# Every other piece of the experts' weights is issued by ScalarE instead of SyncE

## The chip, the cores and the metric

The kernel runs on one core of a Trainium2 chip. The metric is the device time of one execution in microseconds (us). The core has TensorE (PE) for matrix products, VectorE (DVE), ScalarE (ACT), GpSimd (POOL) and SyncE (SP). Each has its own queue of instructions, which it works off in order; a transfer (DMA) is an instruction in the queue of the engine that issues it, and runs on the core's 16 DMA engines once it is issued.

## The reference

One token sequence of 256 rows and 1024 columns, all in float32, runs through a hybrid layer (attention beside a gated delta rule), and then through a second block: two kinds of attention, a mixture of 32 experts of which each token takes four, an added embedding, and a last norm. What matters here is the mixture and what follows it:

```python
logits = xt @ w_router + b_router
top_logit, top_e = lax.top_k(logits, 4)
gate = softmax(top_logit)
# for the tokens xs of one expert e:
hh = xs @ w_gu[e] + b_gu[e]                  # w_gu[e]: 1024 x 2048
glu, lin = jnp.split(hh, 2, axis=-1)
glu = jnp.minimum(glu, 7.0); lin = jnp.clip(lin, -7.0, 7.0)
act = glu * sigmoid(1.702 * glu) * (lin + 1.0)
y = act @ w_dn[e] + b_dn[e]                  # w_dn[e]: 1024 x 1024
# y times its gate is added to the token's row; then, for all tokens:
u = rmsnorm(h, g_ple)
h = h + sigmoid(u @ w_ple_gate) * (p @ w_ple_proj)
out = rmsnorm(h, g_final)
```

An expert has 12 MiB of weights, the 32 of them 384 MiB, and each is read once.

## The kernel before

**Units and pieces.** The experts are worked off in 17 units. Most units are two experts side by side with up to 64 tokens each ("pair"); the first and the one at place 15 hold a single expert. The generator `pieces` gives the weights in the order in which they are needed, in pieces of 1 MiB (128 partitions x 2048 numbers): for unit i the 8 pieces per expert of w_gu, then for unit i - 1 the 4 per expert of w_dn. A pair has 16 and 8, so 24 pieces go by from one unit to the next. With one piece of w_ple_proj at i = 12 (`EMB`) there are 385, p0 to p384. From the fourth expert on, the place of an expert's weights comes from a register: `in_register` loads it from the tile `eidi` on SyncE.

**Slots.** `load` (line 103) puts piece after piece into 15 buffers in turn; the names raw, whi and wlo are the tiles whose room is reused for that. `ahead` fills the first eleven while the router still runs; in `run`, `refill` issues as many pieces as there are free slots after each group of products (`products`, recorded in line 1363). Every piece is issued by SyncE in line 116. A transfer's instruction waits for the product that last read its slot, and, as the eight semaphores for transfers are taken in turn, for the landing of the piece eight before it. So no more than eight are in flight.

**One unit on the engines.** TensorE multiplies the tokens by the w_gu pieces into four accumulators (ph), and ScalarE and VectorE copy those to hs (line 1550). While the products of the w_dn pieces of the unit before run (pm), nothing else is wanted of ScalarE. Behind the last of them comes a boundary: ScalarE writes yh, the result times its gate (line 1452), and VectorE the rest yl (line 1453); TensorE gathers the tokens of the unit after next, which ScalarE copies to xs (line 1386); hs is transposed, and `activation` runs on VectorE and ScalarE (sw, act; lines 1432 to 1443); TensorE adds yh and yl to the tokens' rows (`combine`, ohT), and VectorE to hres (line 1464). Then the next w_gu products start. A scheduler sets the order in which these stand on each engine; it is fixed when the kernel is built.

**The end.** Behind the last unit all engines load a register from novi and branch on it (`further`, a loop for tokens beyond 64 per expert, which these inputs don't enter). The gate projection that follows needs w_ple_gate in four pieces, each split into two parts of less precision: a cast on ScalarE (whi, line 315) and a subtraction on VectorE (wlo, line 316). Its products stand in lines 158 to 160.

Of the kernel before, what the change touches and what calls it, by code (L numbers as in the profile page):

```python
# [15 lines left out]
P = 128  # L16
S = 256
D = 1024
# [49 lines left out]
def tile_net(ctx: ExitStack, tc: tile.TileContext, a: dict, dbg=None):  # L68
    nc = tc.nc
    V, A, G, T, SY = nc.vector, nc.scalar, nc.gpsimd, nc.tensor, nc.sync  # L70
# [30 lines left out]
    def slots():  # L101
        return sum(n_ for _, _, n_ in raws)

    def load(src, kc, n, pool=None, rows="(k p) n -> p k n"):

        if pool is None:
            i = count[0] % slots()
            count[0] += 1
            for pool, name, nb in raws:
                if i < nb:  # L110
                    break
                i -= nb
        else:
            (pool, nb), name = pool, "raw"
        raw = pool.tile([P, 2048], F32, name=name, bufs=nb)
        SY.dma_start(raw[:, :kc * n].rearrange("p (k n) -> p k n", k=kc), src.rearrange(rows, p=P))
        return raw

    def piece(src, kc, n, raw=None, by=None):
# [13 lines left out]
    def rows_piece(W, i, pool=None):  # L133
        nh, k0 = i // 2, (i % 2) * 4
        return load(W[k0 * P:(k0 + 4) * P, nh * 512:(nh + 1) * 512], 4, 512, pool)
# [270 lines left out]
    with ExitStack() as c1:  # L406
# [16 lines left out]
        for i in (2, 1):  # L423
# [3 lines left out]
        rows = [("conv_w", 96), ("gdn_norm_w", 1), ("g_cq_2", 3), ("g_ckv_2", 2),  # L427
                ("g_out_mla_2", 4), ("g_out_sb_2", 4), ("g_attn_2", 8), ("g_ple_2", 8)]
        vr = wk.tile([P, P], F32, name="vrow1")
        at = 0  # L430
        for n, k in rows:
            voff[n] = 16 + at
            src = a[n]
            src = src.rearrange("o t (c p) -> (o t c) p", p=P) if n == "conv_w" else src.rearrange("o (c p) -> (o c) p", p=P)
# [678 lines left out]
    NE = 32  # L1113
# [6 lines left out]
    def pieces(units):  # L1120


        for i in range(len(units) + 1):
            if i < len(units):
                rs = [p["row"]() for p in units[i]["places"]]
                for k in range(8):
                    for r in rs:
                        yield wgu[bass.ds(r + k * P, P)], 1, 2 * D, "(k p) n -> p k n"
            if i:
                rs = [p["row"]() for p in units[i - 1]["places"]]  # L1130
                for q in range(4):
                    for r in rs:
                        yield wdn[bass.ds(r + q * 2 * P, 2 * P)], 2, D, "(p k) n -> p k n"
            if i == EMB:
                yield a["w_ple_proj_2"][0], 2, D, "(k p) n -> p k n"

    def ahead_or_none(order):
        for src, kc, m, rows in order:
            return load(src, kc, m, None, rows), kc, m

    def ahead(order, n, pool=None):

# [2 lines left out]
    def in_register(ap):  # L1145

        r = []

        def row():
            if not r:  # L1150
                r.append(nc.values_load(ap, engines=[mybir.EngineType.SP], min_val=0, max_val=NE - 1) * D)
            return r[0]
        return row

    with ExitStack() as c3:
# [31 lines left out]
        def unit(ps_, i):  # L1187


            return dict(places=ps_, at=i)  # L1190
# [264 lines left out]
        def combine(b, tiles=(0, 1)):  # L1455
            for t in tiles:
                pss = [pm.tile([P, 512], F32, name="pm") for _ in range(2)]
                for nh in range(2):
                    ns = slice(nh * 512, nh * 512 + 512)
                    for i, y in enumerate(b["y"]):  # L1460
                        mm(pss[nh], b["oh"][:, t], y[:, ns], start=i == 0, stop=i == 1)
                for nh in range(2):
                    o = hres[:, t, nh * 512:nh * 512 + 512]
                    V.tensor_tensor(o, o, pss[nh], ALU.add)  # L1464
                yield

        def bias_of(ev):
            br = wk.tile([P, 512], F32, name="sw", bufs=4)[:8, :2 * P]
            SY.dma_start(br, a["b_gu_2"][0].rearrange("e (q f) -> e q f", f=2 * P)[bass.ds(ev, 1)].rearrange("o q f -> (o q) f"))
            ps = pm.tile([P, 2, 8], F32, name="pm")  # L1470
            for k in range(2):
                turn_(ps[:, k], br[:, k::2])
            bi = wk.tile([P, 16], F32, name="bie")
            V.tensor_copy(bi.rearrange("p (q k) -> p k q", k=2), ps)
            return bi
# [132 lines left out]
        def further():  # L1608

            every = raws[:]  # L1610
            raws[:] = raws[:1]
            count[0] = 0
            with tc.If(nov[0] > 0):
                with tc.For_i(0, nov[0]) as jv:
                    ji = wk.tile([P, 2], I32, name="ji")
                    cur = wk.tile([P, 2, 2], F32, name="cur")
                    oh = wk.tile([P, NE], F32, name="oh")
                    x1 = wk.tile([P, NE], F32, name="x1")
                    bs = wk.tile([P, 2], F32, name="bs")
                    jf = wk.tile([P, 1], F32, name="jf")  # L1620
                    V.tensor_copy(jf, iota16[:, bass.ds(jv, 1)])
                    V.tensor_scalar(x1, st0, jf, None, ALU.is_le)
                    V.scalar_tensor_tensor(oh, ce, jf, x1, ALU.is_gt, ALU.mult)

                    V.tensor_scalar(x1, st0, jf, -64.0, ALU.subtract, ALU.mult)
                    V.scalar_tensor_tensor(x1, o0, 64.0, x1, ALU.mult, ALU.add)
                    V.tensor_scalar(x1, x1, 65.0, None, ALU.add)
                    V.tensor_tensor(x1, x1, oh, ALU.mult)
                    V.tensor_reduce(bs[:, 0:1], x1, AX.X, ALU.add)
                    V.tensor_tensor(x1, oh, iota32, ALU.mult)  # L1630
                    V.tensor_reduce(bs[:, 1:2], x1, AX.X, ALU.add)
                    V.tensor_copy(ji, bs)
                    for t in range(2):
                        V.tensor_tensor(x1, oh, selp[:, t], ALU.mult)
                        V.tensor_reduce(cur[:, 0, t:t + 1], x1, AX.X, ALU.add)
                        V.tensor_tensor(x1, oh, gate[:, t], ALU.mult)
                        V.tensor_reduce(cur[:, 1, t:t + 1], x1, AX.X, ALU.add)
                    V.tensor_scalar(cur[:, 0], cur[:, 0], bs[:, 0:1], None, ALU.subtract)
                    ej = nc.values_load(ji[0:1, 1:2], engines=[mybir.EngineType.SP], min_val=0, max_val=NE - 1)
                    bi = bias_of(ej)  # L1640
                    one = [unit([dict(row=lambda: ej * D, v=[lambda t: cur[:, 0, t:t + 1]],
                                      g=lambda t: cur[:, 1, t:t + 1], bias=lambda: bi)], 0)]
                    for _ in combine(run(one, pieces(one), [], None, (("hs", 2), ("hs", 2)))):
                        pass
            raws[:] = every
# [124 lines left out]
```

## Time and profile before

| what | before |
|---|---|
| median of 3 runs | 1566.31 us (1565.58 to 1567.18) |
| the profiled execution | 1564.52 us, of which its span (first to last instruction) 1562.7 us |
| mean granted clock of TensorE | 0.985 |
| TensorE busy | 1427.0 us (91%) |
| VectorE, ScalarE busy | 618.7 us (40%), 415.6 us (27%) |
| transfer queue (SyncE's) | 485.87 MB, 78.3% of 16 engines' span |

The profile is one execution. A share of busy time is a mean over stages that differ: up to about 550 us the hybrid layer, the attention and the router run, from there to about 1520 us the experts, then the embedding's gate and the last norm. Busy time doesn't say what an engine waits for; the lists of waits and the order in time say that, and the slices of the span say in which stage.

### The profile page before, as it was taken

Reading aid. Unit: us, or ns where it says so; the run is one execution under the profiler, and the core shown is the slowest. Engines: PE = TensorE matmul, PEld = TensorE weight load, DVE = VectorE, ACT = ScalarE, POOL = GpSimd, SP = SyncE. Lnnn points to the kernel's source line nnn. Section 1 sums busy time; section 2 is a strip of 40 time slices with the busy share of each in tenths; the row PEclk is TensorE's granted clock in tenths of the full one; section 3 lists DMA queues with packets and bytes.
Section 4 is the critical chain, followed back from the end, with each engine's and each line's share of the span. In section 5 each row is a group of like instructions: output and inputs, shape, how many; then the busy total and the mean of one; then the engine's idle time right before and its main releaser. Section 6 shows DMA issues by size and latency. Waiting matters only on the chain. (4 is left out here: it accounts for less than half of the span.)

```text
span 1562.7 us, 20025 instructions
## 1 busy us (share of the span) xinstructions
PE 1427.0 (91%) x7922; PEld 872.8 (56%) x7922; DVE 618.7 (40%) x1215; ACT 415.6 (27%) x636; POOL 27.1 (2%) x39
## 2 busy tenths in 40 slices
PE   6999998999889999998989988999998899897887
PEld 5889898999788865443433332444343244242235
DVE  6868865556556651330221330231223022122126
ACT  5543654444457521110110110111011011011014
POOL 0000100000000000000000000000000000000000
PEclk9999999999999989999999999999999999999998
DMA  7544244355354199999999999999999999999982
GB/s 241 165 150 150 89 143 130 108 189 201 100 165 136 54 379 393 421 421 421 421 421 420 421 422 421 420 421 421 421 421 421 421 420 422 421 421 421 421 336 88
DMA packets 108541, 487.58 MB, mean 312 GB/s; under 512 B 14766, under 2 KB 23356, under 8 KB 59292
## 3 DMA queue, kind: packets, MB, share of 16 engines
q1 hardware_dynamic: 108300, 485.87, 78.3%
q8 instruction: 64, 1.05, 0.3%
q0 software_dynamic: 144, 0.39, 0.1%
q14 instruction: 33, 0.27, 0.0%
HBM read 483.48 MB, written 2.75 MB: 311 GB/s over the span
## 5 line engine op out<-in xcount | busy, mean ns | idle before, releaser
L1363 PE MATMUL ph<-raw,xs 128*64 128x512 f32 x928 | 233.9, 597 | 7.3 <-DMA raw<-in_w_gu_dram 7.3
L1363 PE MATMUL ph<-whi,xs 128*64 128x512 f32 (+1 forms) x568 | 192.8, 594 | 1.4 <-DMA whi<-in_w_gu_dram 1.3
L316 DVE TENSOR_TENSOR wlo<-raw,whi 128x2048 fp32r<-128x2048 f32 (+4 forms) x73 | 158.0, 2165 | 87.9 <-ACT whi L315 87.7
L1363 PE MATMUL ph<-wlo,xs 128*64 128x512 f32 (+1 forms) x552 | 187.1, 594 | 3.2 <-DMA wlo<-in_w_gu_dram 3.2
L212 PE MATMUL pm<-w,wlo 128*128 128x256 f32 x640 | 179.9, 282 | 6.9 <-DVE wlo L316 6.9
L210 PE MATMUL pm<-w,whi 128*128 128x256 f32 x640 | 182.6, 286 | 3.3 <-ACT whi L315 3.3
L1550 DVE COPY hs<-ph 128x512 f32<-128x512 f32 x34 | 23.5, 691 | 405.4 <-PE ph L1363 405.4
L211 PE MATMUL pm<-w,whi 128*128 128x256 f32 x640 | 180.4, 282 | 0.3 <-DVE w L316 0.3
L315 ACT CAST whi<-raw 128x2048 fp32r<-128x2048 f32 (+4 forms) x73 | 132.0, 1808 | 135.8 <-PE pm L211 83.9
L1363 PE MATMUL pm<-raw,act 128*64 128x512 f32 x528 | 146.3, 597 | 22.7 <-DMA raw<-in_w_dn_dram 22.0
L1363 PEld LDWEIGHTS ph<-raw,xs 128*64 128x64 f32 x928 | 75.0, 138 | 143.0 <-issue 126.1
L1550 ACT COPY hs<-ph 128x512 f32<-128x512 f32 x34 | 19.9, 585 | 413.6 <-PE ph L1363 413.6
L1453 DVE SCALAR_TENSOR_TENSOR yl<-pm,gs,yh 128x512 fp32r<-128x512 f32 x34 | 25.5, 749 | 262.0 <-ACT yh L1452 261.2
L212 PEld LDWEIGHTS pm<-w,wlo 128*128 128x128 f32 x640 | 122.3, 192 | 8.1 <-DVE wlo L316 8.0
L210 PEld LDWEIGHTS pm<-w,whi 128*128 128x128 f32 x640 | 122.2, 191 | 4.1 <-ACT whi L315 3.9
L211 PEld LDWEIGHTS pm<-w,whi 128*128 128x128 f32 x640 | 122.3, 191 | 0.8 <-DVE w L316 0.7
L1363 PEld LDWEIGHTS ph<-whi,xs 128*64 128x64 f32 (+1 forms) x568 | 61.9, 140 | 83.0 <-issue 78.4
L1363 PEld LDWEIGHTS ph<-wlo,xs 128*64 128x64 f32 (+1 forms) x552 | 59.3, 140 | 84.7 <-issue 76.8
L1363 PE MATMUL pm<-wlo,act 128*64 128x512 f32 (+1 forms) x248 | 94.2, 597 | 13.0 <-DMA wlo<-in_w_dn_dram 13.0
L1363 PE MATMUL pm<-whi,act 128*64 128x512 f32 (+1 forms) x248 | 92.4, 596 | 13.2 <-DMA whi<-in_w_dn_dram 13.2
L1363 PEld LDWEIGHTS pm<-raw,act 128*64 128x64 f32 x528 | 44.0, 136 | 102.3 <-issue 59.9
L1452 ACT ACTIVATE yh<-pm,gs 128x512 fp32r<-128x512 f32 x34 | 23.4, 687 | 279.0 <-PE pm L1363 277.2
(394 smaller groups left out, 1921.7 us busy)
## 6 DMA issues: line engine op xcount, KB each, us to landing
raw<-in_w_gu_dram SPq DMA_DIRECT2D x116, 1024.0 KB, 19.8
whi<-in_w_gu_dram SPq DMA_DIRECT2D x71, 1024.0 KB, 19.8
wlo<-in_w_gu_dram SPq DMA_DIRECT2D x69, 1024.0 KB, 19.8
raw<-in_w_dn_dram SPq DMA_DIRECT2D x66, 1024.0 KB, 19.8
raw<-in_w_in_dram SPq DMA_DIRECT2D x46, 1024.0 KB, 5.9
wlo<-in_w_dn_dram SPq DMA_DIRECT2D x31, 1024.0 KB, 19.8
whi<-in_w_dn_dram SPq DMA_DIRECT2D x31, 1024.0 KB, 18.6
raw<-in_w_branch_a_dram SPq DMA_DIRECT2D x4, 1024.0 KB
```

The source lines that it names most:

```text
L210: T.matmul(o, hi[:, k, ns], xh[:, k0 + k], start=first, stop=False)
L211: T.matmul(o, hi[:, k, ns], xl[:, k0 + k], start=False, stop=False)
L212: T.matmul(o, lo[:, k, ns], xh[:, k0 + k], start=False, stop=last)
L315: A.copy(hi, src)
L316: (by or V).tensor_tensor(lo, src, hi.bitcast(F32), ALU.subtract)
L1363: return tc.keep_in_program_order(T.matmul(*x_, **y_))
L1452: A.activation(yh[:, ns], yp[n_], AF.Copy, scale=b["gs"])
L1453: V.scalar_tensor_tensor(yl[:, ns], yp[n_], b["gs"], yh[:, ns].bitcast(F32), ALU.mult, ALU.subtract)
L1550: (V.tensor_copy if j // 2 else A.copy)(b["hs"][j // 2][:, j % 2 * 512:j % 2 * 512 + 512], hp[j])
```

## The change

`load` takes the engine that issues as an argument, and `fetch`, through which `refill` gets its pieces, gives the odd pieces to ScalarE (`A`) and the even ones to SyncE (`SY`). The first eleven pieces stay on SyncE. A register that holds an expert's place is loaded on both engines. No piece's size, slot or place in the order of pieces changes.

```diff
--- before.py
+++ after.py
@@ -101,7 +101,7 @@
     def slots():
         return sum(n_ for _, _, n_ in raws)
 
-    def load(src, kc, n, pool=None, rows="(k p) n -> p k n"):
+    def load(src, kc, n, pool=None, rows="(k p) n -> p k n", by=None):
 
         if pool is None:
             i = count[0] % slots()
@@ -113,7 +113,7 @@
         else:
             (pool, nb), name = pool, "raw"
         raw = pool.tile([P, 2048], F32, name=name, bufs=nb)
-        SY.dma_start(raw[:, :kc * n].rearrange("p (k n) -> p k n", k=kc), src.rearrange(rows, p=P))
+        (by or SY).dma_start(raw[:, :kc * n].rearrange("p (k n) -> p k n", k=kc), src.rearrange(rows, p=P))
         return raw
 
     def piece(src, kc, n, raw=None, by=None):
@@ -1134,9 +1134,16 @@
             if i == EMB:
                 yield a["w_ple_proj_2"][0], 2, D, "(k p) n -> p k n"
 
+
+    turns = [0]
+
+    def fetch(src, kc, m, rows):
+        turns[0] += 1
+        return load(src, kc, m, None, rows, A if turns[0] % 2 else SY), kc, m
+
     def ahead_or_none(order):
         for src, kc, m, rows in order:
-            return load(src, kc, m, None, rows), kc, m
+            return fetch(src, kc, m, rows)
 
     def ahead(order, n, pool=None):
 
@@ -1148,7 +1155,7 @@
 
         def row():
             if not r:
-                r.append(nc.values_load(ap, engines=[mybir.EngineType.SP], min_val=0, max_val=NE - 1) * D)
+                r.append(nc.values_load(ap, engines=[mybir.EngineType.SP, mybir.EngineType.Activation], min_val=0, max_val=NE - 1) * D)
             return r[0]
         return row
 
@@ -1636,7 +1643,7 @@
                         V.tensor_tensor(x1, oh, gate[:, t], ALU.mult)
                         V.tensor_reduce(cur[:, 1, t:t + 1], x1, AX.X, ALU.add)
                     V.tensor_scalar(cur[:, 0], cur[:, 0], bs[:, 0:1], None, ALU.subtract)
-                    ej = nc.values_load(ji[0:1, 1:2], engines=[mybir.EngineType.SP], min_val=0, max_val=NE - 1)
+                    ej = nc.values_load(ji[0:1, 1:2], engines=[mybir.EngineType.SP, mybir.EngineType.Activation], min_val=0, max_val=NE - 1)
                     bi = bias_of(ej)
                     one = [unit([dict(row=lambda: ej * D, v=[lambda t: cur[:, 0, t:t + 1]],
                                       g=lambda t: cur[:, 1, t:t + 1], bias=lambda: bi)], 0)]
```

Of the 374 pieces behind the first eleven, 187 are issued by ScalarE. The scheduler's order on ScalarE, VectorE and SyncE changes with it; line numbers behind line 1137 rise by 7 (line 1452 becomes 1459, 1386 becomes 1393, and so on).

ScalarE at the boundary of two units, in the kernel before:

```order
L1550 COPY hs<-ph 128x512 x2
L1452 ACTIVATE yh<-pm,gs 128x512 x2
L1386 COPY xs<-pm 128x512 x2
L1439 ACTIVATE sw<-sw 128x512
L1443 ACTIVATE act<-sw 128x512
```

The same place now (DMA is the issue of a piece, the ISA ahead of it a part of its waits):

```order
L116 ISA
L116 DMA whi<-in_w_gu_dram 128x2048
L1459 ACTIVATE yh<-pm,gs 128x512
L116 ISA
L116 DMA wlo<-in_w_gu_dram 128x2048
L1459 ACTIVATE yh<-pm,gs 128x512
L1393 COPY xs<-pm 128x512 x2
L1446 ACTIVATE sw<-sw 128x512
L1450 ACTIVATE act<-sw 128x512
```

One issue now stands ahead of the two yh activations and one between them, and the xs copies stand behind both.

ScalarE at the end of the last unit up to the branch, in the kernel before:

```order
L1443 ACTIVATE act<-sw 128x512
L1452 ACTIVATE yh<-pm,gs 128x512 x2
L315 CAST whi<-raw 128x2048
L1605 TENSOR_LOAD novi
L1613 COMPARE_AND_BRANCH
```

The same place now:

```order
L1450 ACTIVATE act<-sw 128x512
L315 CAST whi<-raw 128x2048 x2
L1459 ACTIVATE yh<-pm,gs 128x512 x2
L315 CAST whi<-raw 128x2048
L1612 TENSOR_LOAD novi
L1620 COMPARE_AND_BRANCH
```

One cast of w_ple_gate stood behind yh; now two stand ahead of it and a third behind it, all ahead of the branch.

VectorE at the same place, in the kernel before:

```order
L1441 SCALAR_TENSOR_TENSOR sw<-sw 128x512
L1464 TENSOR_TENSOR hres<-hres,pm 128x512 x3
L1453 SCALAR_TENSOR_TENSOR yl<-pm,gs,yh 128x512 x2
L1605 TENSOR_LOAD novi
L1613 COMPARE_AND_BRANCH
```

And now:

```order
L1448 SCALAR_TENSOR_TENSOR sw<-sw 128x512
L1471 TENSOR_TENSOR hres<-hres,pm 128x512 x3
L316 TENSOR_TENSOR wlo<-raw,whi 128x2048 x2
L1460 SCALAR_TENSOR_TENSOR yl<-pm,gs,yh 128x512 x2
L316 TENSOR_TENSOR wlo<-raw,whi 128x2048
L1612 TENSOR_LOAD novi
L1620 COMPARE_AND_BRANCH
```

Three of the four subtractions for w_ple_gate have moved ahead of the branch, two of them ahead of yl.

## Rows read from the trace of the kernel before

**Rows 1.** The page: GB/s in 40 slices, the transfer queue, issue to landing.

```profile
GB/s 241 165 150 150 89 143 130 108 189 201 100 165 136 54 379 393 421 421 421 421 421 420 421 422 421 420 421 421 421 421 421 421 420 422 421 421 421 421 336 88
...
q1 hardware_dynamic: 108300, 485.87, 78.3%
...
raw<-in_w_gu_dram SPq DMA_DIRECT2D x116, 1024.0 KB, 19.8
```

**Rows 2.** Busy time, granted clock, DMA share and GB/s by stretch; us, counts in brackets.

```profile
core 0: us, PE busy (x) PEld busy (x) DVE busy (x) ACT busy (x) POOL busy (x), PEclk, DMA share, GB/s
564.00:576.00 12.00, 11.04 (x46) 9.63 (x48) 8.91 (x56) 0.74 (x2) 1.18 (x2) 0.50 1.01 403
600.00:605.00 5.00, 5.00 (x29) 2.26 (x30) 3.30 (x10) 1.26 (x2) 0.00 (x0) 1.00 0.74 303
...
610.00:615.00 5.00, 5.00 (x26) 1.72 (x24) 0.00 (x0) 0.00 (x0) 0.00 (x0) 1.00 1.01 426
640.00:840.00 200.00, 183.69 (x868) 75.56 (x869) 49.48 (x110) 21.24 (x34) 0.74 (x1) 0.98 1.01 421
```

**Rows 3.** SyncE's queue, 660 to 1480 us: us waited, times, longest.

```profile
SPq L116 <- DMA raw<-in_w_gu_dram: 163.2, 84, 2.6
...
SPq L116 <- PE ph L1363: 60.9, 48, 8.9
```

**Rows 4.** Line 116, 545 to 640 us: issue duration in ns, min/median/max.

```profile
L116 SPq DMA_DIRECT2D raw<-in_w_gu_dram x19: 327/333/622, 548.7 to 625.8; - x19
```

**Rows 5.** SyncE in time: two issues to a row, landings set the spacing.

```profile
1387.63 2.82 SPq L116 DMA_DIRECT2D whi<-in_w_gu_dram  x2
1392.60 2.81 SPq L116 DMA_DIRECT2D wlo<-in_w_gu_dram  x2
```

**Rows 6.** One unit boundary in time: start, us, engine, operation, wait before it.

```profile
1191.53 0.64 PE L1363 MATMUL pm<-raw,act 128*64 128x512 f32 x1 [1.31 <-DMA raw<-in_w_dn_dram]
...
1194.41 1.49 ACT L1452 ACTIVATE yh<-pm,gs 128x512 fp32r<-128x512 f32 x2 [20.18 <-PE pm L1363]
...
1197.19 0.58 ACT L1386 COPY xs<-pm 128x512 f32<-128x512 f32 x1 [1.29 <-PE pm L1363]
...
1198.78 1.12 PE L1367 MATMUL pm<-C,hs 128*128 128x128 f32 x8
...
1204.77 7.52 PE L1363 MATMUL ph<-raw,xs 128*64 128x512 f32 x34
...
1241.96 3.65 PE L1363 MATMUL pm<-raw,act 128*64 128x512 f32 x16 [1.32 <-DMA raw<-in_w_dn_dram]
```

**Rows 7.** The unit boundary with the embedding: ScalarE's copy, next gate-and-up product.

```profile
1254.82 1.49 ACT L1452 ACTIVATE yh<-pm,gs 128x512 fp32r<-128x512 f32 x2 [20.25 <-PE pm L1363]
...
1273.49 3.65 PE L1363 MATMUL ph<-whi,xs 128*64 128x512 f32 x16
```

**Rows 8.** The end of the experts in time.

```profile
1513.37 0.39 SPq L116 DMA_DIRECT2D raw<-in_w_ple_gate_dram  x1
...
1519.46 1.49 ACT L1452 ACTIVATE yh<-pm,gs 128x512 fp32r<-128x512 f32 x2 [12.33 <-PE pm L1363]
...
1520.18 1.55 DVE L1453 SCALAR_TENSOR_TENSOR yl<-pm,gs,yh 128x512 fp32r<-128x512 f32 x2 [11.92 <-ACT yh L1452]
1520.84 1.89 ACT L315 CAST whi<-raw 128x2048 fp32r<-128x2048 f32 x1
...
1522.84 0.73 PE L1363 MATMUL pm<-yh,ohT 128*128 128x512 f32 x1 [2.63 <-ACTq L1613]
...
1524.65 2.28 DVE L316 TENSOR_TENSOR wlo<-raw,whi 128x2048 fp32r<-128x2048 f32 x1
...
1526.85 0.68 DVE L1464 TENSOR_TENSOR hres<-hres,pm 128x512 f32<-128x512 f32 x1
...
1530.64 0.50 PE L158 MATMUL ph<-whi,raw 128*128 128x512 f32 x1 [1.00 <-ACT whi L315]
```

**Rows 9.** The chain that ended last, at the same place.

```profile
1521.26 5.01 DMA raw<-in_w_ple_gate_dram
```

## The prediction

> **What bounds the kernel now.** I read the page first, for the whole span, then one stretch, then one unit, then the end. From about 600 us on the transfer queue moves 421 GB/s in nearly every slice [rows 1], and in the stretch from 640 to 840 us the DMA engines are busy for all of the time, while TensorE is busy for 183.69 of 200 us [rows 2]. So the experts' weights set the time there, not the products. The reader should check that against the queue: SyncE's longest total of waits is for transfers that landed (163.2 us in 84 waits for one group of pieces alone), more than for a product that frees a buffer (60.9 us) [rows 3]. One issue takes 0.33 us [rows 4], two issues come every 1392.60 - 1387.63 = 4.97 us [rows 5], so a piece of 1 MiB takes 2.485 us, and 19.8 us from issue to landing [rows 1] is 8 pieces in flight. SyncE's work of issuing is about a seventh of its time. Then comes an end of about 40 us, in which no expert's weight is transferred and one operation waits for another [rows 8, 9]; there every microsecond counts.
>
> **What issuing from two engines takes away.** SyncE has half the issues less, 187 x 0.33 = 62 us of its queue, and all of it lies beside transfers, since the next issue waits for the landing of the piece eight before it on the same semaphore. That wait stays, on whichever engine the issue stands. Worth nothing as long as the queue never runs empty. It did run empty once, 600 to 605 us at 303 GB/s [rows 2], and there SyncE waited for a product to free a slot; the slot is freed no earlier in the new kernel. So 0 us is gained.
>
> The Trainium skill, page "DMA: Bandwidth & Descriptors", section "Issuing engines are not separate DMA queues", says that transfers issued by several engines end up on the same 16 DMA engines and that a second issuer saves the issuing time only. The trace's 0.33 us in 2.485 agrees that there is nothing to save; by that rule alone the time would stay where it is, which is the second rival below.
>
> **What it adds at each boundary of two units.** ScalarE now holds about 12 of the 24 issues of a unit, each with a wait in front that ScalarE's own work stands behind. In the order shown ahead, the last issue stands between the two yh activations, and behind it the xs copies. It is for the piece that comes 15 after the last one that TensorE just used, and waits for the one 8 before that, thus for the landing 7 pieces after the last dn piece: 7 x 2.485 = 17.4 us. With 0.4 us for the issue and 0.58 us for the copy, the first xs copy ends 18.4 us after the last dn piece has landed. Before, TensorE went on to the transposes 1198.78 - 1191.53 = 7.25 us after that landing [rows 6]. So TensorE is held up by 18.4 - 7.25 = 11.1 us, less whatever TensorE already lags behind the landings.
>
> What can hide it is TensorE's own slack. A pair of pieces takes it 3.44 us (3.65 us less the overlap at the end) where two landings take 4.97 [rows 5, 6]. The boundary takes from 1191.53 + 3.44 = 1195.0 to 1204.77 = 9.8 us [rows 6]. A unit is 12 x 3.44 + 9.8 = 51 us of TensorE against 24 x 2.485 = 59.6 us of transfers: 8.6 us of slack. A hold-up of 11.1 - x, x being the lag, equals 8.6 at x = 2.5 us. So TensorE should settle at a lag of 2.5 us with no waits for weights left, and stand at most 2.5 + 9.8 + 8.6 + 3.4 = 24 us behind after a boundary: ten landings of the 15 slots, so five are still in flight. The transfers go on at the full rate and the cost is 0. If that cover is gone, each missing microsecond costs 15 us, once per unit. At the unit with the embedding the boundary is longer, from 1255.4 (0.6 us behind the start of yh, as above) to 1273.49 = 18.1 us [rows 7]; with 2.5, 8.6 and 3.4 us on top the lag is 33 us or 13 landings, one or two in flight. There the rate may fall as it did at 600 us, (421 - 303) / 421 x 10 us = 2.8 us at most. I take 0.5 us, nearer to nothing.
>
> The clock can eat the slack. After an idle TensorE the row from 564 to 576 us shows a granted clock of 0.50, the 1.2 GHz level [rows 2]. Twelve microseconds at half speed cost 6 us of products; the slack of 8.6 us still covers it, and the hold-up shrinks as the lag grows, so the two don't add. I take 0 and keep it as a rival.
>
> **What moves at the end.** Behind the last expert products comes a branch that all engines pass. The second and third excerpt show that before, ScalarE had one cast of w_ple_gate in front of the branch and VectorE none; after, ScalarE has two casts in front of yh and a third behind it, and VectorE three subtractions (wlo) in front of it. TensorE's first product behind the branch waits for VectorE to pass it; that came 1522.84 - 1521.73 = 1.1 us after the last yl (1520.18 + 1.55) [rows 8].
>
> Now the same chain in the new order. The second gate piece is issued at 1513.37 [rows 8] and takes 5.0 us like the one on the chain [rows 9]: it lands at 1518.4. ScalarE casts it until 1518.4 + 1.89 = 1520.3, then does yh until 1520.3 + 1.49 = 1521.8 instead of 1520.95, then the third cast until 1523.7. VectorE does the second wlo from 1520.3 to 1522.6 (2.28 us), yl until 1524.1, the third wlo until 1526.4. With 1.1 us for the branch the first product comes at 1527.5 instead of 1522.84: +4.7 us [rows 8]. If the three or four gate pieces share the rate and the second lands as late as 1520.1, the sum is +6.4.
>
> Is it given back? Behind the branch there is less left to do: before, a wlo of 2.28 us stood in front of the second hres, and the projection's products ran through from 1530.64, 7.8 us after the first one [rows 8]. In the new order one wlo (the fourth) still stands between the hres additions and the transposed copy that feeds the projection, so I count again 1.2 + 0.7 + 0.7 for two additions, 2.28 for wlo, two copies and a cast at 0.6 to 0.7 each, and a subtraction: 7.5 to 7.8 us. Little returns, 0 to 1.5 us. TensorE idles about 7 us in front of that product instead of 2.63 [rows 8] and may run longer at half clock; the 6 us of the row at 564 us bounds it, and I take 0.5. The end costs 4.7 - 0.5 + 0.5, about +4.7, between +3 and +10.
>
> **Sum.** 0 for issuing, 0 at the boundaries, 0.5 at the embedding, 4.7 at the end: +5.2 us. The profiled execution, 1564.52 us (its span of 1562.7 and 1.8 around it), becomes 1569.7; on the median of 1566.31, which is 1.8 above it, 1571.5 us.
>
> **The rivals.** A measurement tells 0.2% of this kernel from no change, 3.1 us here.
> *Nothing that can be measured* (1563.2 to 1569.4; 1567 likeliest): the transfers set the time and the casts at the end give their time back, so that less than 3.1 of the 5.2 us is left. For it: the casts and wlos that moved in front of the branch are not done behind it, 3.8 us of ScalarE (2 x 1.89) and 6.8 us of VectorE (3 x 2.28) [rows 8]. Against it: TensorE waits for VectorE there, and its products behind the branch ran without gaps before, so nothing late is caught up.
> *Much slower* (1577 to 1600): the boundaries aren't covered. It decides where TensorE stays at half clock for more than 2 x 8.6 = 17 us in a unit; at 20 us each of 15 units loses 10 - 8.6 = 1.4 us, 21 us in all: 1592. For it: 8.6 us idle per unit is longer than any boundary wait before. Against it: the longest stretch at half clock that I found is the 12 us [rows 2].
> *Faster* (under 1563.2; 1560.5 as worked out): two queues feed the 16 DMA engines better than one. The place is the 374 pieces behind the first eleven, 374 x 2.485 = 929 us; the price is the rate. Short stretches of one queue reach 426 GB/s [rows 2], 1.2% over 421, worth 11 us, 5.2 of which the end takes back: 1560.5. It decides from (5.2 + 3.1) / 929 = 0.9%, 424.8 GB/s. Against it: the engines were already busy all the time, so better feeding has no gap to fill. No row shows two queues in use at once, and the rate could as well fall to the 403 of a busy stretch [rows 2], which I count with the slower rival.
> That ScalarE issues nothing can be left out: its order shows the issues.
>
> **How the numbers follow.** The forecast, +3.1 to +10.7 us (1569.4 to 1577): 0.50. Nothing measurable: 0.20. Much slower: 0.16. Faster: 0.14. So faster 0.14, same 0.20, slower 0.66. The likeliest single case gives 1571.5. For 8 in 10 the range takes the first two (0.70) and reaches into both others: up to 1588, not quite half of the slower one (0.07), and down to 1561, about a third of the faster one (0.05); 0.82 in all.
>
> **What would show it.** GB/s in the slices from 640 to 1480 us should stay at 421 within 2; a lower one means the boundaries starve the queue, a higher one that two queues help. TensorE's waits for landed dn weights (1.32 us a time [rows 6]) should all but go, and waits for ScalarE's xs copies, of some 8 us a unit, take their place. The granted clock at each boundary shows whether 0.50 lasts over 17 us. The last expert products should end near 1520, the first product behind the branch near 1527.5, and the projection run through from about 1535. If the first gate cast ends later than 1520.3, the end was mis-sized; if the last dn products end more than 3 us late, the boundaries were.

## The result and the profile after

The changed kernel takes 1574.59 us (median of 5 runs, 1573.91 to 1578.36), the kernel before 1566.03 us beside it (1563.72 to 1567.18). The ratio is 1.0066, with a 95% interval of 1.0055 to 1.0078: 8.6 us more by the medians, 10.3 by the ratio (0.0066 x 1566), where 5.2 had been forecast. The profiled execution's span is 1572.1 us, 9.4 more than before.

The page of the changed kernel: GB/s in 40 slices, and the two queues.

```profile
GB/s 243 161 156 144 108 124 128 122 193 207 75 189 107 75 414 384 422 420 421 421 421 420 421 421 421 421 354 414 408 420 422 420 414 422 421 421 421 421 366 41
...
q1 hardware_dynamic: 81372, 289.77, 48.0%
q10 hardware_dynamic: 26928, 196.10, 30.2%
```

Against [rows 1]: 196.10 MB went by ScalarE's queue, and two queues at once move 420 to 422 GB/s, the same as one. But from slice 27 on (a slice is 39.3 us, so 1022 us) three slices stand at 354, 414 and 408 where all stood at 420 to 422 before. Time is lost there and hardly anywhere else in the middle.

What TensorE waited for from 660 to 1480 us in the changed kernel: us in total, times, longest.

```profile
PE pm L1374 <- DVE yl L1460: 33.6, 9, 8.3
PE pm L1374 <- ACT xs L1393: 30.9, 9, 4.1
...
PE pm L1370 <- DMA wlo<-in_w_dn_dram: 1.2, 1, 1.2
```

The waits for landed w_dn weights, of the kind at the end of [rows 6], are gone but for one, and 64.5 us of waits for yl and xs ahead of the transposes have come in their place. What ScalarE itself waited for in the same stretch:

```profile
ACT yh L1459 <- DMA raw<-in_w_gu_dram: 89.3, 9, 19.2
ACT yh L1459 <- DMA whi<-in_w_gu_dram: 74.8, 5, 18.8
ACT yh L1459 <- DMA wlo<-in_w_gu_dram: 62.8, 7, 16.3
```

An activation that reads a result of TensorE waits for a transfer of w_gu that it has nothing to do with: it stands behind an issue that waits for that landing. (The idle time begins before the issue could have been due; not all of it is loss.)

One boundary of units in the changed kernel, the one ahead of the unit at place 15 (the places count experts: this unit is the ninth of the 17); start, us, engine, operation, wait before it:

```profile
992.95 0.69 ACT L1459 ACTIVATE yh<-pm,gs 128x512 fp32r<-128x512 f32 x1 [14.39 <-DMA whi<-in_w_gu_dram]
...
997.66 0.34 ACTq L116 DMA_DIRECT2D raw<-in_w_dn_dram  x1
998.04 0.69 ACT L1459 ACTIVATE yh<-pm,gs 128x512 fp32r<-128x512 f32 x1 [4.41 <-DMA wlo<-in_w_gu_dram]
998.63 1.07 ACT L1393 COPY xs<-pm 128x512 f32<-128x512 f32 x2
...
999.26 1.13 PE L1374 MATMUL pm<-C,hs 128*128 128x128 f32 x4 [4.05 <-ACT xs L1393]
...
1004.87 1.45 PE L1370 MATMUL ph<-whi,xs 128*128 128x512 f32 x3
```

The same boundary in the kernel before:

```profile
984.23 1.49 ACT L1452 ACTIVATE yh<-pm,gs 128x512 fp32r<-128x512 f32 x2 [20.65 <-PE pm L1363]
...
987.01 0.59 ACT L1386 COPY xs<-pm 128x512 f32<-128x512 f32 x1 [1.29 <-PE pm L1363]
...
994.49 1.88 PE L1363 MATMUL ph<-whi,xs 128*128 128x512 f32 x4
```

Before, yh starts with the last w_dn product and the next w_gu products follow 10.3 us later. After, the last w_dn product starts at 986.1, the second yh comes 11.9 us behind it, and the next w_gu products 18.8 us behind it.

To see where the 10 us went, I read three more figures from the order in time and from the transfers' bytes, for each kernel: the stretch from the first w_gu product to the start of the last w_dn product, the rest from there to the end, and the time in which the bytes from 250 to 300 MiB moved (about 988 to 1113 us before).

| us | before | after | difference |
|---|---|---|---|
| first w_gu product to last w_dn product | 945.4 | 953.2 | +7.8 |
| last w_dn product to the end | 43.1 | 45.8 | +2.7 |
| 250 to 300 MiB | 124.5 | 132.7 | +8.2 |

The two first sum to +10.5; the first w_gu product itself came 1.2 us earlier in the profiled execution (573.1 against 574.3), which is why the span shows 9.4. So the middle costs nearly eight, in one place, and the end under three.

The end in the changed kernel, against [rows 8]:

```profile
1522.23 1.90 ACT L315 CAST whi<-raw 128x2048 fp32r<-128x2048 f32 x1 [8.38 <-DMA raw<-in_w_ple_gate_dram]
...
1525.98 1.90 ACT L315 CAST whi<-raw 128x2048 fp32r<-128x2048 f32 x1 [1.84 <-DMA raw<-in_w_ple_gate_dram]
...
1527.78 1.26 ACT L1459 ACTIVATE yh<-pm,gs 128x512 fp32r<-128x512 f32 x2
...
1530.12 1.41 DVE L1460 SCALAR_TENSOR_TENSOR yl<-pm,gs,yh 128x512 fp32r<-128x512 f32 x2
...
1531.44 2.28 DVE L316 TENSOR_TENSOR wlo<-raw,whi 128x2048 fp32r<-128x2048 f32 x1
...
1533.92 0.77 PE L1370 MATMUL pm<-yh,ohT 128*128 128x512 f32 x1 [6.99 <-ACT whi L315]
```

The last w_dn product starts at 1526.3, and yh waits behind the second cast until 1527.78. VectorE does yl and then a third wlo, and the first product behind the branch comes 7.6 us behind the last w_dn product. Before it was 3.2.

### The profile page after: what moved, and what is told of

The parts are those of the page before. It is cut to its first block, busy times and chain, and to the rows that moved or that the text cites. A ratio compares the mean times of both kernels' runs of the same rounds, so it can differ in the third digit from the quotient of the medians.

```text
span 1572.1 us, 20043 instructions
## 1 busy us (share of the span) xinstructions
PE 1426.1 (91%) x7922; PEld 888.3 (56%) x7922; DVE 618.7 (39%) x1215; ACT 413.3 (26%) x636; POOL 27.2 (2%) x39
## 3 DMA queue, kind: packets, MB, share of 16 engines
q10 hardware_dynamic: 26928, 196.10, 30.2%
## 5 line engine op out<-in xcount | busy, mean ns | idle before, releaser
L1370 PE MATMUL ph<-raw,xs 128*64 128x512 f32 x928 | 228.2, 596 | 0.0
L1370 PE MATMUL ph<-wlo,xs 128*64 128x512 f32 (+1 forms) x552 | 183.7, 593 | 0.0
L1370 PE MATMUL pm<-raw,act 128*64 128x512 f32 x528 | 137.7, 593 | 2.0 <-DMA raw<-in_w_dn_dram 1.3
L1374 PE MATMUL pm<-C,hs 128*128 128x128 f32 x256 | 50.8, 353 | 53.1 <-ACT xs L1393 26.7
## 6 DMA issues: line engine op xcount, KB each, us to landing
wlo<-in_w_gu_dram ACTq DMA_DIRECT2D x35, 1024.0 KB, 18.9
```

The lines of the kernel that those rows point to most:

```text
L1370: return tc.keep_in_program_order(T.matmul(*x_, **y_))
L1374: return tc.keep_in_program_order(T.transpose(out, in_, ident[:k, :k]))
```

## The experiments

**Theory 1**, formed from the two traces: ScalarE's hold-up at a boundary is hidden by TensorE's slack everywhere but around the unit at place 15; the new order at the end costs the rest. **Theory 2**: two queues, or ScalarE's waits, cost a little at every boundary. The ratios below are against the kernel before, run beside each version; 0.1% is 1.6 us.

### e1: no ScalarE issues around place 15

```diff
-        return load(src, kc, m, None, rows, A if turns[0] % 2 else SY), kc, m
+        return load(src, kc, m, None, rows, A if turns[0] % 2 and not 176 <= turns[0] + 10 < 236 else SY), kc, m
```

> The change, but the 60 pieces p176 to p235 around the unit at place 15 are all issued by SyncE; the new order at the end stays. Theory 1 (the hold-up of ScalarE costs only where TensorE has no slack, ahead of and in the unit at place 15, some 7 us, and the new order at the end costs some 3.5 us): 3 to 4.5 us above the kernel before, 1569 to 1570.5, transfers at 421 GB/s from 1020 to 1120 us. Theory 2 (two queues, or ScalarE's waits, cost a little at every boundary): 157 of 187 issues on ScalarE are left, so 7 to 9 us above, 1573 to 1575.

Measured: 1574.67 us, ratio 1.0056 (1.0035 to 1.0077). Theory 1 missed, and the total is the one that theory 2 expected. Yet the place itself is clean: 250 to 300 MiB take 124.7 us. A loss of 6.9 us has turned up at 1220 to 1240 us, one unit after ScalarE begins to issue again. ScalarE there:

```profile
1148.96 0.63 ACT L1450 ACTIVATE act<-sw 128x512 f32<-128x512 f32 x1 [0.97 <-DVE sw L1448]
1149.34 0.34 ACTq L116 DMA_DIRECT2D whi<-in_w_gu_dram  x1
1150.09 0.34 ACTq L116 DMA_DIRECT2D wlo<-in_w_gu_dram  x1
1150.74 0.92 ACTq L116 DMA_DIRECT2D raw<-in_w_gu_dram  x2
```

Its first four issues stand behind an activation of the boundary, and go out together at 1149 to 1152 us, while SyncE's of the same pairs had gone out from 1130 on. TensorE then reaches the next boundary 13 us late (last w_dn product at 1207.5 us instead of 1194.6), and the hold-up of 10 us comes on top. The gap in ScalarE's issues made a delay of its own, so this run doesn't part the theories.

### e2: only the issues around place 15

```diff
+        return load(src, kc, m, None, rows, A if turns[0] % 2 and 176 <= turns[0] + 10 < 236 else SY), kc, m
```

> Only the odd pieces of p176 to p235 are issued by ScalarE, 30 issues; the order at the end is that of the kernel before. Theory 1: 6 to 9 us above the kernel before, 1572 to 1575, all of it lost between 1000 and 1120 us, where the transfers starve. Theory 2: 30 of 187 issues, so 1 to 2 us above, 1567 to 1568.

Measured: 1564.70 us, ratio 0.9989 (0.9977 to 1.0000). Theory 1 missed again in this form, and theory 2's 1 to 2 us isn't there either. The trace says why: the scheduler put the first of these issues behind the boundary at 988 us, which takes 10.1 us as before; the two boundaries behind it take 11.2 and 12.6 us and cost next to nothing (250 to 300 MiB: 125.2 us). So it isn't the issues in and behind the unit at place 15. What is left of theory 1 is the one boundary ahead of it.

### e3: the last 24 pieces on SyncE

```diff
+        return load(src, kc, m, None, rows, A if turns[0] % 2 and turns[0] + 10 < 361 else SY), kc, m
```

> The change up to p360; the last 24 pieces are issued by SyncE, and with that the casts of w_ple_gate stand at the end as in the kernel before. Theory 1: only the cost in the middle is left, 6 to 8 us above the kernel before, 1572 to 1574, and the first product behind the branch 2.6 us behind the last expert product, as before. If the new order at the end costs nothing, the time is that of the changed kernel, 1574.6.

Measured: 1569.28 us, ratio 1.0026 (1.0013 to 1.0039). The middle is as in the changed kernel (132.7 us for 250 to 300 MiB), and the end is that of before: the first product behind the branch 3.2 us behind the last w_dn product, 42.1 us to the end. The total is 3 us lower than expected: the last units give back part of the loss (+5.1 us to the last w_dn product where the transfers had lost 8.7).

### e4: GpSimd instead of ScalarE

```diff
-        return load(src, kc, m, None, rows, A if turns[0] % 2 else SY), kc, m
+        return load(src, kc, m, None, rows, nc.gpsimd if turns[0] % 2 else SY), kc, m
```

(An excerpt: the registers are loaded on GpSimd for it, in two more lines.)

> The odd pieces are issued by GpSimd instead of ScalarE, so that there are two queues but ScalarE waits for no transfer; the new order at the end stays. Theory 1: no hold-up at any boundary, 3 to 4.5 us above the kernel before for the end alone, 1569 to 1570.5. Theory 2 in its form that two queues cost: 8 to 10 us above, as the changed kernel. If two queues feed the engines better, the rate from 640 to 1480 us is above 421 GB/s and the time below that of before.

Measured: 1567.97 us, ratio 1.0015 (1.0003 to 1.0027), 1 us below theory 1's range. Its page and two stretches (columns as in [rows 2]):

```profile
q1 hardware_dynamic: 81372, 289.77, 47.9%
q0 software_dynamic: 27072, 196.49, 30.1%
```

```profile
640.00:840.00 200.00, 181.68 (x870) 76.60 (x871) 50.87 (x115) 22.49 (x37) 21.34 (x40) 0.98 1.01 421
1040.00:1240.00 200.00, 191.19 (x922) 80.56 (x919) 48.65 (x110) 24.68 (x40) 22.74 (x43) 1.00 1.01 420
```

The same share of the bytes by a second queue, and no loss in the middle: 945.6 us to the last w_dn product, 0.2 more than before. What is left is the end, 45.9 us, +2.8. Two queues cost nothing and bring nothing; what costs in the middle is what stands behind the issues on ScalarE. Theory 2 falls in the form that two queues cost.

### e5: the changed kernel without one boundary

```diff
+        return load(src, kc, m, None, rows, A if turns[0] % 2 and not 166 <= turns[0] + 10 < 190 else SY), kc, m
```

> The change, but the 24 pieces p166 to p189, which are issued around the one boundary ahead of the unit at place 15, are all issued by SyncE; ScalarE keeps 175 of its 187 issues, and the new order at the end stays. Theory 1, mended (ScalarE's hold-up of some 9 us is hidden at every boundary by TensorE's slack, except at the one that the unit at place 15 follows, whose products take 3.4 us per piece and so have no slack): that boundary takes 10 us instead of 19, the transfers stay at 421 GB/s from 1020 to 1120 us, and 3 to 4.5 us for the end are left, 1568.5 to 1570. If the loss comes from two engines issuing and not from that boundary, or only moves to the next boundary, 1573 to 1575.

Measured: 1570.31 us, ratio 1.0032 (1.0016 to 1.0047). With 175 of 187 issues still on ScalarE, half the cost is gone. The boundary takes 10.1 us, and 250 to 300 MiB 127.4 us. The 2.9 that remain there belong, by the order in time, to the boundary after it, which takes 14.0 us instead of 10.7 in the changed kernel. The mended theory 1 holds in the main: the time is just above its range of 1568.5 to 1570, and it had expected no loss there at all.

### e6: the splits at the end held behind the branch

```diff
+                pin[0] = True
                 gate_w[i] = piece(None, 4, 512, gate_w[i])
+                pin[0] = False
```

(An excerpt.) With `pin` set, `split` keeps its cast and its subtraction behind what was written ahead of them on their engines.

> The change, with the second to fourth split of w_ple_gate held behind the branch: ahead of yh stands one cast instead of two and a third behind it, ahead of yl one subtraction instead of three. Theory 1: the boundary ahead of place 15 still costs its 7 to 8 us of transfers, the end costs nothing: first product behind the branch 2.6 to 3.5 us behind the last expert product, 1569 to 1571. If the moved casts weren't what the end costs, 1573 to 1575.

Measured: 1572.17 us, ratio 1.0034 (1.0021 to 1.0047). By the median this is above the range of 1569 to 1571; by the ratio it is 5.3 us more than before. The middle loses as expected (132.8 us). The end takes 41.1 us, 4.7 less than in the changed kernel and 2.1 less than before:

```profile
1528.45 1.90 ACT L318 CAST whi<-raw 128x2048 fp32r<-128x2048 f32 x1 [8.38 <-DMA raw<-in_w_ple_gate_dram]
...
1530.39 2.29 DVE L319 TENSOR_TENSOR wlo<-raw,whi 128x2048 fp32r<-128x2048 f32 x1 [9.18 <-ACT whi L318]
...
1532.40 1.49 ACT L1462 ACTIVATE yh<-pm,gs 128x512 fp32r<-128x512 f32 x2 [2.05 <-PE pm L1373]
...
1533.13 1.55 DVE L1463 SCALAR_TENSOR_TENSOR yl<-pm,gs,yh 128x512 fp32r<-128x512 f32 x2 [0.45 <-ACT yh L1462]
...
1535.79 0.47 PE L1373 MATMUL pm<-yh,ohT 128*128 128x512 f32 x1 [2.63 <-DVEq L1623]
```

yh waits for TensorE alone, and the first product behind the branch comes after 2.63 us of idle time, as in [rows 8]. One split runs beside the last products and holds up nothing. So the second to fourth split, moved ahead of the branch, cost 4.7 us.

### e7: that end in the kernel before

The kernel before, with the four w_ple_gate pieces and the first split written ahead of the last yh and yl, and the other splits pinned as in e6; an excerpt.

```diff
+                    if i == n and hook:
+                        hook()
-                    gated(b, yp, room)
+                    gated(b, yp, room, i == n and hook)
```

> The kernel before, all pieces on SyncE, with another order at the end: the four w_ple_gate pieces are issued ahead of the branch, the first one is split ahead of yh and yl while ScalarE and VectorE are idle, the other three behind the branch. Theory 1 (at the end the splits on ScalarE and VectorE ahead of yh and yl are what costs, and those that fit into idle time save): the second hres comes right behind the first, 2 us earlier than before, 1562.5 to 1564.5. If the casts at the end don't matter, the time of the kernel before, 1565.7.

Measured: 1566.63 us, ratio 1.0001 (0.9988 to 1.0014). No gain. ScalarE at the end:

```profile
1519.96 1.90 ACT L318 CAST whi<-raw 128x2048 fp32r<-128x2048 f32 x1 [11.53 <-DMA raw<-in_w_ple_gate_dram]
1521.77 1.26 ACT L1456 ACTIVATE yh<-pm,gs 128x512 fp32r<-128x512 f32 x2
```

The first piece, issued at 1511.3, lands at 1520.0 only, about where the last w_dn product starts (1520.9), and the cast now stands ahead of yh: 43.8 us to the end, 0.7 more than before.

### e8: ScalarE issues only behind w_gu products

An excerpt; `phase` is 1 behind w_dn products and 0 behind w_gu products.

```diff
+        return load(src, kc, m, None, rows, A if turns[0] % 2 and not phase[0] else SY), kc, m
```

> ScalarE issues the odd pieces only while w_gu products run, 129 of 187; those that follow w_dn products are issued by SyncE, so that no issue stands ahead of yh and xs at a boundary. The new order at the end stays. Theory 1: boundaries of 10 us as before, transfers at 421 GB/s from 640 to 1480 us, and 3 to 4.5 us for the end, 1568.5 to 1570. If it is the two queues or the number of ScalarE's issues, 69% of the change's cost, 1571 to 1573, with a loss in the middle.

Measured: 1572.51 us, ratio 1.0041 (1.0027 to 1.0056). By the total, theory 1 missed, and the time lies where the number of issues (130 by the trace) would have put it; but the loss in the middle that goes with that isn't there. The middle is as theory 1 expected (boundaries of 10.0 to 10.2 us, 250 to 300 MiB in 125.1 us, 872.2 us for 100 to 450 MiB where before took 871.6), and so is the end (45.6). But TensorE comes to the last w_dn product 4.2 us later. In the last units the scheduler put an issue behind yh:

```profile
1444.27 1.49 ACT L1460 ACTIVATE yh<-pm,gs 128x512 fp32r<-128x512 f32 x2 [19.94 <-PE pm L1371]
1445.28 0.34 ACTq L116 DMA_DIRECT2D whi<-in_w_gu_dram  x1
```

This issue waits for TensorE, through yh, where SyncE would have sent the piece off earlier. TensorE's last w_dn product of a unit comes 3.6 to 5.2 us later than before from 929 to 1259 us and some 6 us later from 1324 us on, though the bytes up to 450 MiB moved in 0.6 us more. That the odd pieces come late by this is my reading of the order; no run parted it from other causes.

### e9 and e10: one boundary more or less

```diff
+        return load(src, kc, m, None, rows, A if turns[0] % 2 and turns[0] + 10 < 190 else SY), kc, m
```

```diff
+        return load(src, kc, m, None, rows, A if turns[0] % 2 and turns[0] + 10 < 166 else SY), kc, m
```

> ScalarE issues the odd pieces only up to p189, 85 of 187, so the last boundary that it holds up is the one ahead of the unit at place 15; everything behind is SyncE's, and the end is that of the kernel before. Theory 1: that one boundary takes 19 us and the transfers lose some 7 us between 1020 and 1070 us as in the changed kernel: 1570 to 1573. If the cost goes with the number of issues on ScalarE or of held boundaries, 45% of it: 1567 to 1569, with no loss at that place.

> As the run up to p189, but only up to p165, 73 issues: the boundary ahead of the unit at place 15 is free again, the six ahead of it are held up as in the changed kernel. Theory 1: those six take 16 to 24 us each and cost nothing, no loss of transfers from 1020 to 1120 us: 1564.5 to 1566.5, the time of the kernel before. If held boundaries cost, 1567 to 1569.

Measured: e9 1571.27 us, ratio 1.0046 (1.0030 to 1.0063); e10 1562.86 us, ratio 0.9983 (0.9970 to 0.9996). ScalarE issues 90 pieces in e9 and 78 in e10 by the traces, a few more than expected ahead of the runs. Twelve issues more, and 8.4 us more. Two stretches of e9 (columns as in [rows 2]):

```profile
1020.00:1040.00 20.00, 20.00 (x59) 8.05 (x59) 1.38 (x2) 1.17 (x2) 0.00 (x0) 1.00 0.97 366
1060.00:1080.00 20.00, 20.00 (x96) 6.70 (x94) 2.24 (x7) 0.21 (x1) 0.00 (x0) 1.00 0.85 349
```

The same two of e10:

```profile
1020.00:1040.00 20.00, 20.00 (x77) 7.30 (x77) 1.39 (x2) 1.17 (x2) 0.00 (x0) 1.00 1.01 421
1060.00:1080.00 20.00, 20.00 (x93) 6.71 (x88) 1.38 (x2) 1.17 (x2) 0.00 (x0) 1.00 1.01 422
```

The boundaries (us from the start of the last w_dn product to the first of the next w_gu products; the time at the head is that of before):

| | 686 | 743 | 924 | 984 | 1035 | 1195 | 250 to 300 MiB |
|---|---|---|---|---|---|---|---|
| before | 10.2 | 10.2 | 10.2 | 10.1 | 10.2 | 10.2 | 124.5 |
| after | 18.4 | 19.3 | 19.0 | 18.8 | 10.7 | 18.0 | 132.7 |
| e5 | 18.6 | 18.9 | 18.8 | 10.1 | 14.0 | 18.7 | 127.4 |
| e9 | 18.4 | 19.0 | 18.8 | 18.8 | 10.2 | 10.2 | 132.3 |
| e10 | 18.5 | 19.0 | 18.8 | 10.1 | 10.2 | 10.2 | 124.8 |

Six held boundaries cost nothing in e10, and the seventh costs 7.5 us in e9. (The first of the six, at 635 us, takes 11.6 us instead of 10.2, the others 16 to 24.) Theory 1, mended, has both (e10 a little below what it expected), and a cost that goes by the number of issues or of boundaries falls. e10 is even 0.17% below the kernel before (0.04 to 0.30); that is less than the 0.2% that is told from no change here, and I have no mechanism for it.

### e11: a shorter look-ahead

```diff
-                while len(ready) < slots() - 1:
+                while len(ready) < slots() - 3:
```

> The change, with pieces issued 12 ahead instead of 14; the 15 slots stay. By the prediction's step the hold-up at a boundary is the look-ahead less the eight in flight, so two landings (5 us) shorter: ordinary boundaries take 13 to 16.5 us instead of 18.8. If ScalarE's work itself, or its queue, is what delays the boundary, it stays at 18 to 19 us. The time may go either way, as there is less room for TensorE's lag ahead of the unit at place 15: 1572 to 1577.

Measured: 1574.61 us, ratio 1.0058 (1.0041 to 1.0076). The boundaries still take 18.4 to 18.7 us, against my expectation. The scheduler's order had changed with it: behind the second hs copy and ahead of xs stand five issues now, where there were four. ScalarE at the second of these boundaries:

```profile
747.46 0.34 ACTq L116 DMA_DIRECT2D wlo<-in_w_gu_dram  x1
752.42 0.34 ACTq L116 DMA_DIRECT2D whi<-in_w_gu_dram  x1
752.87 1.26 ACT L1459 ACTIVATE yh<-pm,gs 128x512 fp32r<-128x512 f32 x2 [18.95 <-DMA raw<-in_w_gu_dram]
757.30 0.34 ACTq L116 DMA_DIRECT2D wlo<-in_w_gu_dram  x1
757.68 1.07 ACT L1393 COPY xs<-pm 128x512 f32<-128x512 f32 x2 [3.55 <-DMA raw<-in_w_gu_dram]
```

The last issue ahead of xs is the 40th of ScalarE, for p89, in this kernel as in the changed one (756.73 us there). So the scheduler put in front of xs the issue that the shorter look-ahead should have moved behind it, and the chain (issue, landing, issue, copy) kept its length. The run says nothing on what a shorter look-ahead would give.

### e12: the end once more

As e7, with the third and fourth w_ple_gate piece issued behind the branch; an excerpt.

```diff
+        pin[0] = True
+        gate_w.extend(rows_piece(a["w_ple_gate_2"][0], i, big) for i in (2, 3))
+        pin[0] = False
```

> The kernel before, with the first w_ple_gate piece split ahead of yh and yl, the second one issued ahead of the branch and the third and fourth behind it, as before. In the run with all four issued ahead of the branch the first one landed 8.7 us after its issue instead of some 5, behind the last expert product, and took the gain away. Theory 1: with two in flight it lands at some 1515 to 1517, the first product behind the branch comes 3.2 us behind the last expert product, and the stretch from there to the end is 1.5 to 2.5 us shorter: 1563 to 1564.5. If not, the time of the kernel before.

Measured: 1567.10 us, ratio 1.0012 (0.9999 to 1.0025). No gain again, and not for the reason that I gave: with two pieces in flight the first still lands 8.7 us after its issue (1510.33 to 1519.02, where the cast starts).

```profile
1519.02 1.90 ACT L320 CAST whi<-raw 128x2048 fp32r<-128x2048 f32 x1 [11.52 <-DMA raw<-in_w_ple_gate_dram]
```

No version among these is 0.2% faster than the kernel before.

## Why the prediction was right, and where its sum was not

The way and the range (1561 to 1588) were right, and the time fell in the likeliest case, 3.1 us above the forecast of 1571.5. But that it fell there is in good part luck: of the +5.2 worked out, 4.7 were for the end and 0.5 for the middle; measured were +2.7 and +7.8. The end was taken too high, and the middle, where most of the cost lies, at next to nothing. The prediction's own sign says so: the last w_dn product came 6.7 us late, where more than 3 was to mean that the boundaries were mis-sized.

- **Issuing from two engines takes nothing away.** Right. The rate stays at 420 to 422 GB/s wherever nothing starves, with ScalarE's queue and with GpSimd's (e4). What the Trainium skill says in "DMA: Bandwidth & Descriptors", section "Issuing engines are not separate DMA queues", that transfers of several issuers end on the same DMA engines, agrees with the 420 and 421 GB/s of e4.
- **The hold-up at a boundary.** Right in place and size: 9.8 + 8.6 = 18.4 us were worked out, 18.4 to 19.3 measured at 686, 743, 924 and 984 us (the table of e9 and e10). This length is the unit's transfers less its products; it says only that the hold-up uses up the slack. The chain itself was shorter than the prediction's: at 745 us the last issue ahead of xs is for p89, 14 pieces behind the last one used (p75) and not 15, and it comes 14.9 us, six landings and not seven, behind the issue that waited for p75 (741.82 to 756.73). The waits for landed w_dn weights went as said; those that replaced them fall on yl as much as on xs.
- **That it costs nothing.** Right for ordinary boundaries: six held ones cost 0 (e10). Wrong for one, and this is the step that was mis-sized: "A unit is 12 x 3.44 + 9.8 = 51 us of TensorE against 24 x 2.485 = 59.6 us of transfers: 8.6 us of slack" was taken for every unit. The unit at place 15 holds one expert, whose products take 27 us for 8 w_gu pieces, as long as a pair's for 16. So TensorE has 51 us of work there and only 16 pieces, 40 us, land meanwhile. The view that shows it is the busy time by stretch of the kernel before:

```profile
1000.00:1100.00 100.00, 97.80 (x408) 44.43 (x408) 24.57 (x55) 12.48 (x20) 0.00 (x0) 1.00 1.01 421
```

TensorE is busy for 97.80 of 100 us there, where [rows 2] shows 183.69 of 200 for an ordinary stretch. The unit behind it has none either: 20 pieces, 49.7 us, against 51.2 us of TensorE (1035.4 to 1086.6), which fits the 2.9 us that e5 still lost at the boundary between the two. A lag that enters this stretch stays. In the changed kernel the 8.7 us carried through: the next last w_dn product came at 1045.8 us instead of 1035.4, where 1.7 of the 10.4 had been there ahead of the boundary. The slots then free so late that the transfers run out:

```profile
1020.00:1040.00 20.00, 20.00 (x66) 7.85 (x66) 1.38 (x2) 1.17 (x2) 0.00 (x0) 1.00 0.95 356
1060.00:1080.00 20.00, 20.00 (x96) 6.71 (x94) 0.47 (x3) 0.00 (x0) 0.00 (x0) 1.00 0.95 383
```

SyncE's queue from 1000 to 1080 us in the kernel before, the longest wait for slots and for landings (30 us each in all):

```profile
SPq L116 <- PE ph L1363: 22.8, 10, 7.9
SPq L116 <- DMA wlo<-in_w_gu_dram: 9.7, 5, 1.9
```

The same in the changed kernel, nearly all of it for products that free slots:

```profile
SPq L116 <- PE ph L1370: 55.9, 10, 13.2
SPq L116 <- PE pm L1370: 11.6, 4, 3.0
SPq L116 <- DMA wlo<-in_w_gu_dram: 4.7, 2, 4.4
```

This term was 0 and measured 8.2 us in the transfers. e9 and e10, which part at that one boundary, show that it is this one.
- **The embedding.** The longer boundary became 27.2 us instead of 18.5, and the transfers lost 0.6 us behind it; 0.5 had been taken.
- **The clock.** It fell to 0.50 behind nearly all held boundaries, for 3 to 10 us each, as in the stretch below, less than the 12 us counted with; e10 has five such stretches and lost nothing. Ahead of the unit at place 15 it was 0.50 from 996 to 1002 us and 1.00 again from 1003 to 1020, and the next w_gu products start 5.2 us behind the xs copies (999.70 to 1004.87), where it was 5.1 before (989.39 to 994.49); so the loss there isn't the clock's.

```profile
754.00:763.00 9.00, 5.21 (x22) 4.50 (x21) 4.69 (x11) 2.83 (x5) 0.00 (x0) 0.50 1.02 422
```

- **The end.** The forecast had +4.7 for the first product behind the branch; it came 4.4 us later behind the last w_dn product than before (7.6 against 3.2). Of that 1.7 came back by the end, where 0 to 1.5 had been allowed and 0.5 taken: +2.7. The order of the chain was right; two sizes in it were not. The 1.1 us from VectorE's last operation to the first product were read where VectorE wasn't what held it ([rows 8] names ScalarE's queue, with a cast that ends 0.11 us before): in the changed kernel wlo ends at 1533.72 and the product starts at 1533.92, 0.20 us later, and it is 0.20 or 0.21 in every version where VectorE is late (e1, e4, e5, e7, e8, e11, e12), while the others show the same 2.63 us of idle time behind TensorE's own last product. And the second w_ple_gate piece took 5.9 us to its cast (1520.09 to 1525.98) instead of 5.0. Against the same end without the moved second to fourth split (e6) these cost 4.7, so the rest of the new order saves 2.1. By the order in time that is the first split, run beside the last products, whose wlo no longer stands between two hres additions; no run shows it by itself, since in e7 and e12 the piece came too late.
- **The rivals.** "Much slower" had the right mechanism, boundaries that aren't covered, and the wrong trigger: no clock of 17 us, but one stretch with no slack. "Faster" is refuted by the rate.

## What to carry to other kernels

An engine that issues transfers takes over their waits, and everything behind an issue in its queue waits for a landing that it doesn't need; here an engine that was idle (GpSimd) was the better second issuer than one whose work others wait for, and with the transfer rate as the bound neither gained. Slack must be worked out for each unit, not for the typical one: look for the stretch in which the engine that is to absorb a delay is busiest, since a delay ahead of it is not absorbed. And read how a changed order moves work far from the edit: here a scheduler that saw other times put other work ahead of a branch.

## What the runs showed that I had not expected

- Two queues of two engines, and even one that GpSimd feeds by software, move the same 420 to 422 GB/s as one.
- The first w_ple_gate piece needed 8.7 us from its issue to its cast where SyncE's queue alone had carried the experts' pieces (e7, e12), and 5.6 us in the changed kernel (1516.67 to 1522.23), with the same sizes; in the six other versions in which two engines issue up to the end it was 5.1 to 6.6. In e7 with four in flight and in e12 with two it was the same 8.7, so their number isn't the cause; what is stays open.
- A rearrangement that only takes issues away from ScalarE in the middle (e1) cost as much as it saved, because the first issue after the gap stood behind an activation.
